# One PSUM ring for scores, transpositions, sums and broadcasts, and a query projection that is asked for first

## The chip, the core and the metric

The program runs on one core of a Trainium2 chip. TensorE (PE) multiplies matrices into PSUM, a small memory of eight banks; ScalarE (ACT) and VectorE (DVE) read the banks and write SBUF; GpSimd (POOL) does some elementwise work; SyncE's queue (SP) issues most DMAs. Each engine works through its own list of instructions in order and waits for others by semaphores. The metric is the device time of one execution in microseconds; lower is better.

## The reference

Two transformer blocks on 512 image positions and, in the second block, 256 context positions, all in float32. The first block mixes a dilated-window and a neighbourhood attention (8 heads of 64 each) and ends in a gated convolutional feed-forward layer. The second block has two layers, and each layer has three attentions, whose outputs are gated, projected and summed:

```python
    ya_l = sweep_query_blocks(lambda i, qb: dense_attend(qb, mk_all, mv_all), mq_l).reshape(b, n, BRANCH_W)
    ...
    yb_l = diff_post(sweep_query_blocks(lambda i, qb: diff_attend(qb, dk_all, dv_all, lam), dq_l),
                     diff_subln, lam_init)
    ...
    yc_l = swa_latent(sq_l, sk_l, sv_l, sk_c, sv_c, swa_sink)

    x = x + gate * merge_branches((ya_l, yb_l, yc_l), z_l, gm_l, w_branch, w_out)
```

The first (in the kernel `mla`) is dense attention of 8 heads over compressed keys. The second (`diff`) subtracts one softmax from another. The third (`swa`) has 16 heads with a window of 128 positions each way plus all of the context, and a learned sink in the softmax. In layer 0 the context's own queries are computed too; in layer 1 they are not.

## The kernel before

Activations lie transposed, 128 channels by positions. A product in float32 is done as three products of split numbers: `mm3` multiplies high by high, low by high and high by low part (L338 to L340). So a projection of 128 outputs over 1024 inputs is 24 matmuls of 512 columns, accumulated in one PSUM bank of the tag `mm`, and a function `evac` then empties it.

An attention is cut into units: one head and two tiles of 128 queries. A unit has two halves. `scores` multiplies queries by keys into banks of the tag `s`, takes the maximum, exponentiates, and scales the rows by the reciprocal sum, which leaves two tiles `p` in SBUF. `values` (L637) transposes `p` in groups of up to 512 columns: PE writes four 128x128 transpositions to a bank `t` (L657), ACT copies it to `pth` and DVE the rest to `ptl` (L381, L382). Then PE multiplies the values by `pth` and `ptl` into the bank `pv` (L675). In `swa` a unit of image queries has three score tiles (two local ones of 256 or 384 columns, L1573 on DVE, and one of both query tiles against the context, L1576) and three transposition groups; a unit of context queries has one of each.

`attend` (L420) writes the work down in this order: the first two transposition groups of the unit before, then the scores of this unit, then portions of other projections, then the products with the values and the third transposition group. The other projections are those of the next head (`mand`) and the gates of the attention (`opt`, functions `gm` and `zz` in `gates`). I call them the fill: they don't depend on the softmax that is under way. A gate `zz` waits for its head's output. When the fill of an attention is used up, what follows on PE is the merge of the branch (L1250), whose sums need every head.

This written order isn't what the engines get. The framework's scheduler goes through it with a model of durations, and takes at each point the instruction written earliest among those that are ready and whose tiles have a free buffer. Buffers of one tag form a ring with a fixed number, and are handed out in the written order. The result is one fixed list for each engine. With the tags as they stand, the eight banks are `mm` 3, `t` 1, `pv` 1 and `s` 3. The tag `t` also serves the sums over channels (`tok_sum`, L551), the tag `s` the broadcasts (`bcast`, L581), and, where `self.wide` is set, every second projection.

In `mla`, `prep` writes down a head's projections: for an even head the keys (`uk`), the values (`ux`) and then the queries (`uq`), for an odd one the queries alone. Their pages of SBUF come from a ring of 11 with the tag `hl`.

Of the kernel before, what the change touches and what calls it, by code (L numbers as in the profile page):

```python
# [9 lines left out]
F32 = mybir.dt.float32  # L10
# [8 lines left out]
P = 128  # L19
# [129 lines left out]
def _vec_layout():  # L149

    lay, off = {}, 0
    for name, n in (("c", 8), ("b_ada", 48), ("g_mix", 8), ("g_ffn", 8), ("g_final", 8), ("c_2", 8), ("c_ctx_2", 8), ("b_mod_2", 48), ("norm_g_2", 16),
                    ("mla_q_norm_2", 6), ("mla_kv_norm_2", 4), ("diff_subln_2", 2), ("final_norm_2", 8)):
        lay[name] = (off, n)
        off += n
    return lay, off
# [92 lines left out]
class Weight:  # L249


    def __init__(self, prog, name):
        self.p, (self.off, self.n), self.parts = prog, prog.U[name], {}
# [25 lines left out]
class Prog:  # L279
    def __init__(self, tc, A, out, stage=None):  # L280
        self.tc, self.nc, self.A, self.out, self.stage = tc, tc.nc, A, out, stage
        self.n = 0
        off, self.U = 0, {}
        for name, w, _ in _units():
            self.U[name] = (off, w)
            off += w * P
        self.lay, self.nvec = _vec_layout()
        self.bg, self.ahead, self.late = [], {}, []
        self.wide, self.turn = False, 0
        self.cur = None  # L290
        self.banks = dict(mm=3, t=1, pv=1, s=3)
        self.lo = self.nc.vector
        self.spare = 0

# [3 lines left out]
        return pool.tile(shape, dt, tag=tag, name=f"{tag}_{self.n}", bufs=bufs)  # L298

    def ps(self, tag):  # L300
        if tag == "mm" and self.wide:

            self.turn += 1
            tag = ("mm", "s")[self.turn % 2]
        return self.t(self.pp, [P, 512], F32, tag, self.banks[tag])

    def page(self):

# [27 lines left out]
    def mm3(self, ps, wh, wl, xh, xl, first, last):  # L336
        mm = self.nc.tensor.matmul
        mm(ps, wh, xh, start=first, stop=False)  # L338
        mm(ps, wl, xh, start=False, stop=False)  # L339
        mm(ps, wh, xl, start=False, stop=last)  # L340
# [944 lines left out]
    def mla(self, l, h, ctx):  # L1285
# [3 lines left out]
        ys, done, st = [], set(), {}  # L1289
# [3 lines left out]
        lat, gens = [], []  # L1293
        for nm, ng, tc_ in (("qc", 3, ctx), ("kvc", 2, True)):
            xs = [self.f3() for _ in range(ng)]
            gens += [self.proj(f"{nm}{l}_{i}", h, lambda ps, cs, x=xs[i]: nc.scalar.activation(x[:, cs], ps, AF.Copy),
                               ctx=tc_, back=l == 0 and tc_) for i in range(ng)]
# [40 lines left out]
        qn, kvn = nrm  # L1338
# [7 lines left out]
        def prep(j):  # L1346
            g, e = j // 2, j % 2
            gens = []
            if e == 0:
                def ev_k(ps, cs):  # L1350
                    self.split_page(kt[0], ps[:64], cs, rows=slice(0, 64))
                    self.split_page(krp, ps[64:], cs, rows=slice(64, P))
                gens.append(self.proj(f"uk{l}_{g}", kvn, ev_k, kn=2, ctx=True))
                st["v", g] = [self.page() for _ in range(2)]
                gens.append(self.v_wide(f"ux{l}_{g}", kvn, st["v", g], 2))
            q = st["q", j] = self.page()
            ys.append(self.f3())

            def ev_q(ps, cs):
                a = self.st()[:, :ps.shape[-1]]  # L1360
                if cs.start == 0:
                    nc.vector.tensor_tensor(a, ps, tab[e], op=ALU.mult)
                else:
                    nc.scalar.activation(a, ps, AF.Copy, scale=self.cmask[:, e:e + 1])
                self.split_page(q, a, cs)

            gens.append(self.proj(f"uq{l}_{j}", qn, ev_q, kn=3, ctx=ctx))
            if e:

                nc.gpsimd.tensor_copy(kt[1][64:], krp[64:])  # L1370
            return gens

        def unit(j, q0, lt):
# [11 lines left out]
            def values():  # L1385
# [4 lines left out]
                if q0 in (256, S):  # L1390
# [5 lines left out]
            return scores, values  # L1396

        heads = [(lambda j=j: prep(j), (8900 if j % 2 else 8900), [unit(j, *q) for q in self.qpairs(ctx)])
                 for j in range(KD)]
        self.run_pairs(heads[0][0]())  # L1400
# [361 lines left out]
```

## Time and profile before

| What | us |
|---|---|
| median of 3 runs | 3541.15 (3540.62 to 3547.24) |
| the profiled execution, its own time | 3543.59 |
| its span, first to last instruction | 3541.7 |
| PE busy | 3421.3 (97%) |
| DVE busy | 2357.5 (67%) |
| ACT busy | 1810.4 (51%) |
| POOL busy | 442.8 (13%) |

The profile gives for every instruction its engine, its source line, its tiles, its start and its duration. Matmuls are pipelined: each one's duration is longer than its distance to the next, so a PE that is busy all the time may still leave small gaps. Times in the rows are counted from the span's start.

### The profile page before, as it was taken

To read this page: it belongs to the slowest core of one execution; us is meant where nothing else is said; L and a number is where in the kernel's file an instruction comes from. 1 tells how busy PE (TensorE), PEld (TensorE's weight loads), DVE (VectorE), ACT (ScalarE), POOL (GpSimd) and SP (SyncE) were. 2 spreads that over 40 slices of the span, in tenths; PEclk is the share of its full clock that TensorE was granted. 3 is DMA by queue.
4 is the path that set the end of the run, shared out by engine and by line. 5 is a ranking of instruction groups with operands and counts; after the bars stand their busy time and mean duration, and the time that the engine had idled before them with its cause. 6 is when DMAs were issued, how large, how long until landed. Compare 5 with 4: busy or idle time off the path is not lost. (4 is left out here: it accounts for less than half of the span.)

```text
span 3541.7 us, 54478 instructions
## 1 busy us (share of the span) xinstructions
PE 3421.3 (97%) x19696; PEld 2926.8 (83%) x19696; DVE 2357.5 (67%) x4964; ACT 1810.4 (51%) x4162; POOL 442.8 (13%) x314
## 2 busy tenths in 40 slices
PE   6999999999999999999999999999999999999998
PEld 4787788778888988899888888888888888887777
DVE  7867678896445546566746777655565666757885
ACT  3456444423556525444525777334673555537772
POOL 3001036652001100001100001000010001000010
PEclk9999999999999999999999999999999999999999
DMA  6844445574211243322252111423114333262224
GB/s 227 261 157 117 157 155 161 165 227 138 75 57 37 60 141 90 85 75 79 56 168 89 58 51 46 145 94 99 56 50 147 111 102 84 77 183 77 63 70 142
DMA packets 200352, 392.41 MB, mean 111 GB/s; under 512 B 26290, under 2 KB 39858, under 8 KB 200083
## 3 DMA queue, kind: packets, MB, share of 16 engines
q1 hardware_dynamic: 199378, 385.23, 35.9%
q0 software_dynamic: 704, 3.70, 0.3%
q8 instruction: 155, 2.54, 0.3%
q14 instruction: 115, 0.93, 0.1%
HBM read 302.82 MB, written 38.83 MB: 96 GB/s over the span
## 5 line engine op out<-in xcount | busy, mean ns | idle before, releaser
L338 PE MATMUL mm<-h,whi 128*128 128x512 f32 (+2 forms) x2748 | 993.4, 362 | 4.2 <-ACT h L611 2.7
L339 PE MATMUL mm<-h,wlo 128*128 128x512 f32 (+2 forms) x2748 | 992.2, 361 | 5.0 <-DVE wlo L275 2.7
L340 PE MATMUL mm<-h,whi 128*128 128x512 f32 (+2 forms) x2748 | 990.1, 361 | 0.0
L274 ACT ACTIVATE whi<-wraw 128x512 fp32r<-128x512 f32 x761 | 470.2, 623 | 569.4 <-PE mm L340 338.5
L275 DVE TENSOR_TENSOR wlo<-wraw,whi 128x512 fp32r<-128x512 f32 (+2 forms) x631 | 445.0, 710 | 309.8 <-ACT whi L274 305.1
L339 PEld LDWEIGHTS mm<-h,wlo 128*128 128x128 f32 (+1 forms) x2748 | 522.0, 190 | 68.6 <-DVE wlo L275 3.3
L338 PEld LDWEIGHTS mm<-h,whi 128*128 128x128 f32 (+1 forms) x2748 | 522.0, 190 | 67.7 <-ACT h L611 3.0
L340 PEld LDWEIGHTS mm<-h,whi 128*128 128x128 f32 (+1 forms) x2748 | 521.9, 190 | 66.0
L382 DVE TENSOR_TENSOR ptl<-t,pth 128x512 fp32r<-128x512 f32 (+1 forms) x480 | 298.1, 621 | 156.4 <-ACT pth L381 151.9
L381 ACT ACTIVATE pth<-t 128x512 fp32r<-128x512 f32 (+1 forms) x480 | 260.5, 543 | 221.5 <-PE t L657 215.7
L657 PE MATMUL t<-ident,p 128*128 128x128 f32 x1680 | 287.3, 280 | 29.9 <-DVE ptl L382 19.5
L657 PEld LDWEIGHTS t<-ident,p 128*128 128x128 f32 x1680 | 195.2, 141 | 96.4 <-DVE ptl L382 44.8
L275 POOL TENSOR_TENSOR wlo<-wraw,whi 128x512 fp32r<-128x512 f32 (+1 forms) x130 | 216.9, 1684 | 262.5 <-ACT whi L274 253.3
L338 PE MATMUL mm<-hl,whi 128*128 128x512 f32 (+1 forms) x680 | 243.0, 358 | 6.3 <-ACT hl L381 5.3
L339 PE MATMUL mm<-hl,wlo 128*128 128x512 f32 (+1 forms) x680 | 240.9, 355 | 0.0
L675 PE MATMUL pv<-pth,hl 128*128 128x256 f32 (+1 forms) x1184 | 224.4, 293 | 6.0 <-ACT pth L381 4.8
L1417 POOL TENSOR_TENSOR st<-st,tab 128x512 f32<-128x512 f32 x52 | 75.1, 1444 | 1198.5 <-DMA st<-st 811.2
L675 PEld LDWEIGHTS pv<-pth,hl 128*128 128x128 f32 x1184 | 178.5, 190 | 48.8 <-ACT pth L381 34.8
L1245 POOL TENSOR_TENSOR f<-f,st 128x512 f32<-128x512 f32 x72 | 85.9, 1194 | 783.9 <-DVE st L1244 606.2
L340 PE MATMUL mm<-f,whi 128*128 128x512 f32 (+1 forms) x504 | 178.3, 355 | 0.0
L1213 ACT ACTIVATE p<-s,m 128x512 f32<-128x512 f32 x192 | 132.1, 688 | 89.9 <-DVE m L1208 88.1
L675 PE MATMUL pv<-ptl,hl 128*128 128x256 f32 (+1 forms) x768 | 169.1, 294 | 1.5 <-DVE ptl L382 1.5
(266 smaller groups left out, 6379.6 us busy)
## 6 DMA issues: line engine op xcount, KB each, us to landing
wraw<-in_wst SPq DMA_DIRECT2D x734, 256.0 KB, 2.7
mraw<-in_w_mod SPq DMA_DIRECT2D x48, 512.0 KB, 3.8
hl<-hl SPq DMA_DIRECT2D x128, 192.0 KB, 3.0
mraw<-in_w_ada SPq DMA_DIRECT2D x36, 512.0 KB, 4.6
tg<-st SPq DMA_DIRECT2D x64, 256.0 KB, 2.0
st<-st SPq DMA_DIRECT2D x208, 64.0 KB, 2.0
p<-tg SPq DMA_DIRECT2D x40, 256.0 KB, 2.8
p<-tg SPq DMA_DIRECT2D x24, 384.0 KB, 3.5
```

Of the source, the lines that this page charges most:

```text
L274: nc.scalar.activation(hi[:, :n], raw[:, :n], AF.Copy)
L275: p.lo.tensor_tensor(lo[:, :n], raw[:, :n], hi[:, :n].bitcast(F32), op=ALU.subtract)
L338: mm(ps, wh, xh, start=first, stop=False)
L339: mm(ps, wl, xh, start=False, stop=False)
L340: mm(ps, wh, xl, start=False, stop=last)
L381: nc.scalar.activation(dst_h, src, AF.Copy)
L382: nc.vector.tensor_tensor(dst_l, src, dst_h.bitcast(F32), op=ALU.subtract)
L657: self.nc.tensor.transpose(tp[:, o + i * P:o + i * P + P], pp[t][:, cols[i]:cols[i] + P], self.ident)
L675: mm(dst, sv, x_[:, o:o + w], start=first, stop=last)
L1213: nc.scalar.activation(p[:, 0:S], a[t], AF.Exp, bias=m[:, 2 + t:3 + t], accum_out=m[:, 4 + t:5 + t])
L1245: nc.gpsimd.tensor_tensor(ys[j][:, cs], ys[j][:, cs], th, op=ALU.mult)
L1417: nc.gpsimd.tensor_tensor(a, a, tab[0], op=ALU.mult)
```

## The change

The tag `t` is given up. Its tiles come from the ring of `s`, which gets the bank and has four. So six tiles of an image unit of `swa` (two transposition groups, three score tiles, a third group) go through four banks in the written order, where before three went through one and three through three. In `wide` stretches the alternation is between three banks and four. In `mla`, the page of the queries is taken before the pages of the values, and `uq` is the first of a head's projections.

```diff
-        self.banks = dict(mm=3, t=1, pv=1, s=3)
+        self.banks = dict(mm=3, pv=1, s=4)
...
     def ps(self, tag):
         if tag == "mm" and self.wide:
             self.turn += 1
             tag = ("mm", "s")[self.turn % 2]
-        return self.t(self.pp, [P, 512], F32, tag, self.banks[tag])
+        self.n += 1
+        ring = "s" if tag == "t" else tag
+        return self.pp.tile([P, 512], F32, tag=ring, name=f"{tag}_{self.n}", bufs=self.banks[ring])
...
         def prep(j):
             g, e = j // 2, j % 2
             gens = []
+            q = st["q", j] = self.page()
             if e == 0:
...
                 st["v", g] = [self.page() for _ in range(2)]
                 gens.append(self.v_wide(f"ux{l}_{g}", kvn, st["v", g], 2))
-            q = st["q", j] = self.page()
             ys.append(self.f3())
...
-            gens.append(self.proj(f"uq{l}_{j}", qn, ev_q, kn=3, ctx=ctx))
+            gens.insert(0, self.proj(f"uq{l}_{j}", qn, ev_q, kn=3, ctx=ctx))
```

The three extracts that follow are from the lists that the scheduler made, with the tiles' full names; the first number in a name is the same in both programs. They show the `swa` of layer 1 late in its course. The first is PE's list before. `s_6941` to `s_6943` are the scores of one unit, and `t_6934` is the first transposition group of the unit ahead of it, whose softmax left `p_6923` and `p_6924`; `mm_6927` is fill, a gate's projection.

```order
L675 MATMUL pv_6912_35157<-ptl_6918_35173,hl_6251_32077 128x256 x2
L1186 MATMUL s_6941_35281<-hl_6229_31911,hl_6799_34656 128x256
L1186 MATMUL s_6942_35282<-hl_6229_31911,hl_6799_34656 128x384
L1186 MATMUL s_6943_35283<-hl_6229_31911,hl_6799_34656 128x256 x2
...
L338 MATMUL mm_6927_35227<-h4_4772_24409,whi_6947_35313 128x512
L339 MATMUL mm_6927_35227<-h4_4772_24409,wlo_6948_35314 128x512
L675 MATMUL pv_6912_35157<-ptl_6933_35244,hl_6251_32077 128x128
L657 MATMUL t_6934_35262<-ident_2_69,p_6923_35188 128x128
L340 MATMUL mm_6927_35227<-h4_4772_24409,whi_6947_35313 128x512
L657 MATMUL t_6934_35262<-ident_2_69,p_6924_35189 128x128
```

Here the scores of the next unit stand ahead of the transpositions of this one, and fill stands between. The second is PE's list after the change, the same tiles:

```order
L660 MATMUL t_6934_35262<-ident_2_69,p_6924_35189 128x128
L660 MATMUL t_6937_35271<-ident_2_69,p_6924_35189 128x128
L1189 MATMUL s_6941_35281<-hl_6229_31911,hl_6799_34656 128x256
L1189 MATMUL s_6942_35282<-hl_6229_31911,hl_6799_34656 128x384
L1191 MATMUL s_6941_35281<-hl_6230_31912,hl_6799_34656 128x256
L1191 MATMUL s_6942_35282<-hl_6230_31912,hl_6799_34656 128x384
L678 MATMUL pv_6912_35157<-pth_6935_35267,hl_6252_32078 128x256 x2
L1189 MATMUL s_6943_35283<-hl_6229_31911,hl_6799_34656 128x256 x2
...
L678 MATMUL pv_6912_35157<-ptl_6951_35333,hl_6251_32077 128x128
L660 MATMUL t_6958_35365<-ident_2_69,p_6944_35292 128x128
```

Both first transposition groups now stand ahead of the next unit's scores, and no projection stands between; the lines are three higher in this program. The third is DVE's list after the change for the same unit, from its first score tile to the scaled rows. `ISA` is the reduction of a local score tile, with its accumulator read.

```order
L1577 ISA p_6944_35292,m_6940_35280<-s_6941_35281,wmask_5_75 128x256
L385 TENSOR_TENSOR ptl_6936_35268<-t_6934_35262,pth_6935_35267 128x512
L385 TENSOR_TENSOR ptl_6939_35277<-t_6937_35271,pth_6938_35276 128x512
L1577 ISA p_6945_35293,m_6940_35280<-s_6942_35282,wmask_5_75 128x384
L1580 TENSOR_REDUCE m_6940_35280<-s_6943_35283 128x2
L385 TENSOR_TENSOR ptl_6951_35333<-t_6949_35330,pth_6950_35332 128x128
L1582 TENSOR_TENSOR m_6940_35280<-m_6940_35280 128x2
L1583 TENSOR_SCALAR m_6940_35280<-m_6940_35280,sink1_6226_31906 128x2
L1596 RECIPROCAL m_6940_35280<-m_6940_35280 128x2
L1601 TENSOR_SCALAR p_6944_35292<-p_6944_35292,m_6940_35280 128x256
```

The two copies of the transposition groups stand between the unit's first score tile and its second.

## Rows read from the trace of the kernel before

**Rows 1.** The page: the span, and PE's busy time, share and instructions.

```profile
span 3541.7 us, 54478 instructions
PE 3421.3 (97%) x19696; PEld 2926.8 (83%) x19696; DVE 2357.5 (67%) x4964; ACT 1810.4 (51%) x4162; POOL 442.8 (13%) x314
```

**Rows 2.** Waits of PE, whole span: waiting line, releaser, us, times, longest.

```profile
PE t L657 <- DVE ptl L382: 19.5, 30, 1.4
PE s L586 <- DVE rstd L578: 10.4, 5, 4.9
```

**Rows 3.** Stretches: length, then busy us (instructions) of each engine, PE clock, DMA.

```profile
930.00:1245.00 315.00, 310.50 (x2025) 276.88 (x2024) 167.47 (x312) 192.22 (x436) 26.29 (x22) 1.00 0.20 59
1880.00:2250.00 370.00, 357.38 (x2271) 307.61 (x2270) 269.00 (x710) 264.63 (x727) 25.65 (x23) 1.00 0.21 62
2190.00:2250.00 60.00, 58.49 (x374) 50.19 (x373) 46.62 (x112) 40.38 (x108) 6.37 (x6) 1.00 0.30 95
3190.00:3455.00 265.00, 256.84 (x1444) 204.17 (x1443) 213.88 (x577) 201.89 (x549) 19.99 (x15) 1.00 0.23 70
3410.00:3450.00 40.00, 38.63 (x214) 29.57 (x213) 31.95 (x81) 26.57 (x74) 3.87 (x3) 1.00 0.29 86
```

**Rows 4.** Waits of PE in 1880 to 2250, then in 3190 to 3455.

```profile
PE t L657 <- DVE ptl L382: 7.9, 10, 1.2
...
PE t L657 <- DVE ptl L382: 3.6, 9, 0.7
```

**Rows 5.** Timeline of PE near 1404: start us, us, engine, line, tiles, shape, count.

```profile
1404.11 0.28 PE L371 MATMUL mm<-whi,h 128*128 128x256 f32 x1
1404.23 0.40 PE L338 MATMUL mm<-h,whi 128*128 128x512 f32 x1
1404.47 0.40 PE L339 MATMUL mm<-h,wlo 128*128 128x512 f32 x1
...
1406.80 0.60 PE L657 MATMUL t<-ident,p 128*128 128x128 f32 x4
```

**Rows 6.** Groups by shape, DVE, 3200 to 3450: busy us, mean ns, idle before.

```profile
L382 DVE TENSOR_TENSOR ptl<-t,pth 128x512 fp32r<-128x512 f32 x61 | 42.0, 688 | 15.0 <-ACT pth L381 14.5
...
L1576 DVE TENSOR_REDUCE m<-s 128x2 f32<-128x512 f32 x30 | 20.5, 683 | 0.8 <-PE s L1188 0.6
...
L1573 DVE CUSTOM_DVE_ANT_0 p<-s,wmask 128x384 f32<-128x384 f32 x29 | 16.0, 550 | 4.0 <-PE s L1188 3.8
...
L1573 DVE CUSTOM_DVE_ANT_0 p<-s,wmask 128x256 f32<-128x256 f32 x29 | 12.1, 416 | 2.5 <-PE s L1188 2.4
...
L382 DVE TENSOR_TENSOR ptl<-t,pth 128x128 fp32r<-128x128 f32 x31 | 8.9, 286 | 0.9 <-ACT pth L381 0.4
L1579 DVE TENSOR_SCALAR m<-m,sink 128x2 f32<-128x2 f32 x30 | 7.6, 252 | 0.3
```

**Rows 7.** Timelines of ACT and DVE: exponentials and scaling of one `swa` unit.

```profile
3321.57 0.28 ACT L1581 ACTIVATE m<-m,sink 128x2 f32<-128x2 f32 x1
3322.65 0.62 ACT L1587 ACTIVATE p<-p,m 128x384 f32<-128x384 f32 x1
...
3324.25 0.16 DVE L1592 RECIPROCAL m<-m 128x2 f32<-128x2 f32 x1
...
3324.50 0.91 ACT L621 ACTIVATE p<-p,m 128x256 f32<-128x256 f32 x2
```

**Rows 8.** Stretches near 465 (columns as in rows 3), and PE's timeline there.

```profile
430.00:461.00 31.00, 29.82 (x179) 26.39 (x177) 16.41 (x36) 10.30 (x18) 0.00 (x0) 1.00 0.41 129
461.00:472.00 11.00, 5.11 (x22) 4.83 (x23) 10.29 (x36) 6.08 (x15) 0.00 (x0) 0.55 0.31 92
...
461.90 0.38 PE L338 MATMUL mm<-h,whi 128*128 128x256 f32 x1 [1.99 <-ACT h L611]
468.28 1.22 PE L586 MATMUL s<-ident,rstd 128*128 128x128 f32 x4 [4.89 <-DVE rstd L578]
```

## The prediction

> **What bounds the kernel now.** I read the page's busy times first: PE works for 3421.3 of 3541.7 us [rows 1], so a change can gain at most the 120 us in which PE stands still, and part of that is the start and the end. Then PE's waits: the largest is of the transpositions (L657) for the copy that empties their one bank, 19.5 us in 30 waits; the next, of the broadcasts (L586) for DVE's `rstd`, is one for data [rows 2]. So the single bank `t` costs what can be seen as 19.5 us, of which 7.9 and 3.6 us lie in the two `swa` stages [rows 4] and 8.0 elsewhere. Then the stages: in `swa` of layer 0 PE is busy for 357.4 of 370 us, in that of layer 1 for 256.8 of 265, and in their last stretches for 58.49 of 60 and 38.63 of 40 us [rows 3]. PE has work up to the end of each, because the fill lasts that long.
>
> **What the change moves.** The two lists of PE decide this case. In every `swa` unit of the list before but a few, the scores of the next unit stand ahead of this unit's transpositions (90 of 90 score tiles in layer 1, 103 of 109 in layer 0); after the change it is none, in any stage. The ring hands out its banks in the written order, and six tiles of a unit go through four banks. So the third score tile needs the bank that the copy of the first transposition group leaves, and that group needs the softmax of its own unit. Where before the softmax of two units ran side by side, each unit now has to finish its softmax before the next unit's scores can begin.
>
> While there is fill this costs little: the scheduler puts more fill into each unit, and attention falls back in the list. Measured in PE work at the same tile, it lags by 29 us in `swa` of layer 0 and by 33 us in layer 1; in all the other attentions the lag ends within 5 us of zero. Then the fill is gone. In layer 1, from the first row of `s_6897` to the last of `s_7039`, eight units, the list after has not one projection among its rows, the list before 96. In layer 0, from `s_4445` to `s_4558`, it is 2 rows against 100. What follows is the merge, which needs all heads. There nothing hides the chain, and PE waits in each unit.
>
> **The price of a unit without fill.** I follow one image unit in the order after, from the end of the row scaling of `p_6924` to that of `p_6945`:
> - a hop and the last four transpositions, 0.60 by the row of four, together 0.65 us [rows 5];
> - the first local score tile, whose two products stand first and third of four: some 0.4 us until DVE can start, by the 0.12 us from one 256-column product to the next [rows 5] and the pipeline's end;
> - on DVE the 256-column tile, two 512-column copies, the 384-column tile: 0.42 + 2 x 0.69 + 0.55 = 2.35 us by mean durations; back to back an instruction starts about 0.08 us before the former's end, so 2.05 [rows 6];
> - the reduction of the third tile 0.68, a 128-column copy 0.29 and two small operations 0.4 [rows 6]: some 1.35;
> - ACT's exponentials to the reciprocal: from 3321.57 to 3324.25, 2.68 us [rows 7];
> - reciprocal to the end of the two scalings: 3324.25 to 3324.50 + 0.91, 1.16 us [rows 7].
>
> Sum: 8.3 us a unit. PE's own work in it is nine transpositions at 0.11, eight score products (six at 0.12, two at some 0.175) and ten value products at 0.12: 3.2 us. So PE waits for 5.1 us a unit. A context unit has one score tile and one group: 0.65 + 0.75 for its scores, a copy of the unit before in between (0.6), 1.1 for reduction and small operations, 1.4 and 1.16 for the two last steps; 5.6 us, of which PE works 1.9.
>
> Layer 1: eight intervals between units, 8 x 8.3 = 66.4 us, less the work in them (3.7 and seven times 3.2, 26.1): 40 us. Layer 0: six intervals behind image units, 49.8 less 20.1 of work, and three behind context units, 16.8 less 6.5: 40 us. Together 80 us. The idle time that these last stretches have already, 1.5 and 1.4 us [rows 3], goes off: 77.
>
> **The clock.** Near 462 us PE waited for 1.99 and 4.89 us within 11 us in which it was busy for 5.11; the granted clock of that stretch was 0.55, after 1.00, and a broadcast's four matmuls took 1.22 us instead of 0.60 [rows 5, 8], so PE was at 1.2 GHz. Waits of 5 us in each unit should bring that about. On the chain it doubles the transpositions and the scores, some 0.9 us a unit, 15 us over 17 units if it lasts through both stretches; I take half, 7.5. The Trainium skill (TensorE: Matmul & The Clock Gate, Part 1: The HAM clock gate) has it that the array runs at 1.2 GHz after idling and at 2.4 GHz after sustained work; by that the whole of both stretches would be slow, and the sum 7.5 us higher. The rows above agree in kind, and nothing here depends on the page.
>
> **What is gained.** The 8.0 us of waits for the bank `t` outside `swa` go. Of the 11.5 us inside, I count half as gone: the third score tile now waits for the same copies, in some hundred places of the list. The worst is that none goes; the best that all the 19.5 do, and the small gaps beside them that don't show as waits.
>
> **The rest.** A projection of queries asked for first moves nine matmuls (18 with context) ahead of the keys and values, and its weight's load, ACT's and DVE's split of it, and the load's place in SP's queue with it. PE has other fill there: it idles for 4.5 us in all of 930 to 1245 [rows 3]. I take 0; it can't give more than those 4.5, and if the values' copies then come late, it costs the latency of such a copy, under 3 us a layer. The fourth bank of `wide` stretches and the sums over channels in the ring: 0, since they wait for data; at most 2 us either way.
>
> **Sum.** 77 + 7.5 - 8.0 - 5.75 = 71 us over the profiled execution's 3543.6 us, 3614. That execution stands 2.4 us above the median, so 3612 us.
>
> **Rivals.**
> - *The ring does what a ring of banks is for* (faster). All waits for the bank go, and the stretches without fill cost nothing, since PE's queue holds what it needs. Time: 3541 - 19.5 = 3522. For it: the waits are real and the largest of PE. Against it: the lists, in which a unit's transpositions always stand ahead of the next scores. It decides if a unit's chain is no longer than its PE work, 3.2 us; the exponentials and scalings alone are 3.84 us [rows 7]. The Trainium skill (Perfetto Trace Analysis, Optimizing Tensor Performance: Matmuls) advises that independent matmul groups rotate through different banks, so that emptying one overlaps the next group; by it this rival would be the likely one. The waits in rows 2 agree with the rule; the order of the lists speaks against its use here. Chance 0.06.
> - *The chain is short.* Without other work between them the steps are faster, with the copies beside the chain: 6.9 us a unit (8.3 less the two copies at 0.6 and 0.2 of overlap). The 14 image intervals then cost 20 us less, the clock stays high, and all bank waits go: 77 - 20 - 19.5 = 38, so 3579. Chance 0.16.
> - *The chain is late everywhere.* Where there is fill, its own copies on ACT and DVE stand between the steps, and the scheduler's durations are too short by some 0.5 us a unit; over some 55 units ahead of the two stretches that is 28 us more, and the clock is low throughout (7.5): 3612 + 36 = 3648. It would show as many waits of transpositions for `p` in the first parts of `swa`. Chance 0.18.
> - *Nothing is to be seen.* Gains elsewhere and losses cancel, to within 0.2%, 7 us, which is about what a measurement of this kernel can tell from no change. It asks for a chain under 4.5 us. Chance 0.05.
>
> **How the numbers follow.** The forecast, 3612 with its own range of 3590 to 3635, has 0.55. The range of 0.8 takes in most of the short chain and of the late one: 3562 to 3660. Slower by over 0.2% are the forecast, the short chain and the late chain, 0.89; within 0.2%: 0.05; faster: 0.06.
>
> **What would show it.** Right: in the two last stretches of `swa`, some 66 us each, PE is busy for less than half and its transpositions wait for ACT's scaling (L621 before, L624 after) some 4 to 5 us each; the granted clock falls there; waits of transpositions for `ptl` are few; the other stages keep their lengths within 3 us. Wrong: PE is busy in those stretches as in rows 3; or the scores' third tile, not the transpositions, is what waits; or the time is lost in the dense part, or in `mla`.

## The result and the profile after

The changed kernel takes 3656.27 us (3652.28 to 3657.6, four runs), beside 3544.19 us for the kernel before on the same chip: a ratio of 1.0315, with a 95% interval of 1.0302 to 1.0328. It is 112 us slower. The forecast was 3612 us, 71 us slower, with a range up to 3660.

First the page of the kernel after: span, busy times, and the clock that PE was granted, in 40 slices of 91 us.

```profile
span 3655.8 us, 54462 instructions
PE 3460.3 (95%) x19696; PEld 2982.8 (82%) x19696; DVE 2376.7 (65%) x4964; ACT 1805.3 (49%) x4162; POOL 443.6 (12%) x314
PEclk9999999999999999999999997999999999999979
```

PE executes the same 19,696 matmuls as before and is busy for 39 us longer [rows 1]. Its clock has two dents, in the slices at the end of the two `swa` stages. Next PE's waits in the whole span (waiting line, releaser, us, times, longest), where rows 2 had the wait for the one bank of the transpositions at the top:

```profile
PE t L660 <- ACT p L624: 76.4, 43, 5.4
PE s L589 <- DVE rstd L581: 10.7, 6, 4.9
PE pv L678 <- DVE ptl L385: 7.8, 13, 2.5
```

The old wait (transpositions for `ptl`, the single bank) has left the head of the list. In its place PE's transpositions wait for ACT's scaling of the rows, four times as long. The same view, restricted to the end of `swa` in layer 0 (2195 to 2300) and in layer 1 (3470 to 3565), has most of it:

```profile
PE t L660 <- ACT p L624: 29.3, 11, 5.4
...
PE t L660 <- ACT p L624: 28.1, 9, 4.3
```

And the stretches (length, busy us and instructions of each engine, PE's clock, DMA): the two ends of `swa`, the two dense parts ahead of them, and `mla` of layer 0.

```profile
2216.70:2287.00 70.30, 41.39 (x185) 37.17 (x185) 37.98 (x107) 35.81 (x105) 2.01 (x2) 0.68 0.07 22
3477.00:3548.00 71.00, 43.43 (x204) 40.60 (x205) 38.55 (x121) 38.25 (x112) 2.54 (x2) 0.72 0.02 6
1888.00:2200.00 312.00, 300.54 (x1896) 259.66 (x1895) 214.81 (x558) 211.58 (x578) 22.91 (x19) 1.00 0.20 57
3260.00:3470.00 210.00, 203.28 (x1118) 166.79 (x1116) 159.28 (x418) 149.57 (x402) 18.23 (x12) 1.00 0.26 75
935.00:1255.00 320.00, 311.23 (x2019) 279.27 (x2018) 167.88 (x310) 191.01 (x434) 25.37 (x22) 0.99 0.20 58
```

Where before PE was busy for 58.49 of 60 us and 38.63 of 40 [rows 3] (the 60 run some 16 us into the merge; in the 70 ahead of it PE is busy for 67.55), it is now busy for 41.39 of 70.30 and 43.43 of 71.00 us, and that at a mean clock of 0.68 and 0.72. The dense parts are as before: in layer 0 11.5 us idle in 312 here, 11.1 in 310 before (370 - 357.38 less 60 - 58.49, rows 3); in layer 1 6.7 in 210 here, 6.8 in 225 before (265 - 256.84 less 40 - 38.63).

To place the whole difference I take the start of the same projection tile in both traces, at the borders of the stages (start after minus start before, so the growth within a stage is a difference of two; with another projection as the border it shifts by some us, for `mla` 1 of the changed kernel between 8 and 13):

| Kernel | `mla` 0 | `swa` 0 | `mla` 1 | `swa` 1 | at 3510 us, in all |
|---|---|---|---|---|---|
| the changed kernel | +7.5 | +47.7 | +11.0 | +43.7 | +113.8 |
| queries first, alone | +4.9 | -1.2 | +8.2 | +0.9 | +10.9 |
| changed, scores written first | +1.9 | -10.8 | +2.6 | -7.9 | -23.6 |
| changed, ring of five | +22.7 | +43.7 | +23.4 | +43.8 | +134.9 |
| `mm` 2, `t` 2 | +21.6 | -6.9 | +27.1 | -3.3 | +47.5 |
| `mm` 2, one bank unused | +22.9 | -0.2 | +35.5 | +6.0 | +77.0 |
| changed, no scaling in the last heads | +5.1 | +20.6 | +9.9 | +25.3 | +63.4 |

So 91 of the 114 us arise in `swa` and 18.5 in `mla`; `diff`, the first block and the merges have the rest.

One unit of the end of layer 1, step by step. This is the timeline of the kernel after (start, us, engine, line, tiles, shape, count), shortened to the steps of the chain:

```profile
3505.78 0.90 ACT L624 ACTIVATE p<-p,m 128x256 f32<-128x256 f32 x2
...
3506.33 1.97 PE L660 MATMUL t<-ident,p 128*128 128x128 f32 x8 [3.34 <-ACT p L624]
3507.95 0.88 PE L1189 MATMUL s<-hl,hl 128*128 128x384 f32 x2
...
3508.75 1.29 DVE L385 TENSOR_TENSOR ptl<-t,pth 128x512 fp32r<-128x512 f32 x2 [1.79 <-ACT pth L384]
...
3509.59 0.70 PE L1189 MATMUL s<-hl,hl 128*128 128x256 f32 x2
3509.96 0.55 DVE L1577 CUSTOM_DVE_ANT_0 p<-s,wmask 128x384 f32<-128x384 f32 x1
...
3510.78 0.69 DVE L1580 TENSOR_REDUCE m<-s 128x2 f32<-128x512 f32 x1
...
3512.36 0.29 ACT L1585 ACTIVATE m<-m,sink 128x2 f32<-128x2 f32 x1 [0.69 <-DVE m L1583]
...
3514.88 0.17 DVE L1596 RECIPROCAL m<-m 128x2 f32<-128x2 f32 x1
...
3515.14 0.91 ACT L624 ACTIVATE p<-p,m 128x256 f32<-128x256 f32 x2 [0.49 <-DVE m L1596]
```

The steps are scaling, transpositions, the first scores, the copies that empty the banks, DVE's reduction of the first score tile (3509.96, behind its two copies, though the products were done by 3509.37), that of the third tile (whose products begin at 3509.59, after the first of the two copies into `ptl`), exponentials, reciprocal, scaling. Each waits for one ahead of it, by data or by its engine's order. From the end of one second scaling (3505.78 + 0.90) to the next (3515.14 + 0.91) it takes 9.37 us, and PE waits 3.3 us for it.

### The profile page after: what moved, and what is told of

Same layout as the page of the kernel before. It is cut to its first block, busy times and chain, and to the rows that moved or that the text cites. A ratio compares the mean times of both kernels' runs of the same rounds, so it can differ in the third digit from the quotient of the medians.

```text
span 3655.8 us, 54462 instructions
## 1 busy us (share of the span) xinstructions
PE 3460.3 (95%) x19696; PEld 2982.8 (82%) x19696; DVE 2376.7 (65%) x4964; ACT 1805.3 (49%) x4162; POOL 443.6 (12%) x314
## 5 line engine op out<-in xcount | busy, mean ns | idle before, releaser
L343 PEld LDWEIGHTS mm<-h,whi 128*128 128x128 f32 (+1 forms) x2748 | 520.5, 189 | 70.3
L660 PE MATMUL t<-ident,p 128*128 128x128 f32 x1680 | 276.4, 292 | 90.2 <-ACT p L624 76.4
L385 DVE TENSOR_TENSOR ptl<-t,pth 128x512 fp32r<-128x512 f32 (+1 forms) x480 | 285.1, 618 | 114.6 <-ACT pth L384 110.9
L384 ACT ACTIVATE pth<-t 128x512 fp32r<-128x512 f32 (+1 forms) x480 | 244.9, 543 | 230.7 <-PE t L660 220.3
L660 PEld LDWEIGHTS t<-ident,p 128*128 128x128 f32 x1680 | 203.9, 149 | 138.0 <-ACT p L624 102.8
L1189 PE MATMUL s<-hl,hl 128*128 128x256 f32 (+2 forms) x640 | 188.9, 364 | 8.6 <-DVE ptl L385 5.7
```

The source lines that it names most:

```text
L384: nc.scalar.activation(dst_h, src, AF.Copy)
L385: nc.vector.tensor_tensor(dst_l, src, dst_h.bitcast(F32), op=ALU.subtract)
L660: self.nc.tensor.transpose(tp[:, o + i * P:o + i * P + P], pp[t][:, cols[i]:cols[i] + P], self.ident)
L1189: mm(ps, q[:, par, q_], k[:, par, k_], start=st[0], stop=False)
```

## The experiments

Ratios are to the kernel before, run beside each on the same chip, with 95% intervals.

**1. The edit on queries alone**, on the kernel before:

```diff
+            q = st["q", j] = self.page()
             if e == 0:
...
-            gens.append(self.proj(f"uq{l}_{j}", qn, ev_q, kn=3, ctx=ctx))
+            gens.insert(0, self.proj(f"uq{l}_{j}", qn, ev_q, kn=3, ctx=ctx))
```

> Before, with the queries' projection asked for first and nothing else: the ring of four is undone. My theory (the loss comes from the common ring alone, which puts each unit's transpositions ahead of the next unit's scores): 3544 us, within 4 us of before in each direction, both mla stages within 3 us of before. Rival (the later values of mla cost the 8 us and 11 us that the two mla stages grew by): 3560 to 3566 us, with the growth in the two mla stages and none in swa.

3555.01 us, 1.0033 (1.0021 to 1.0046): some 10 to 12 us, all in the two `mla` (table), between my range and the rival's. My "0" was wrong. Which half of the edit does it, experiments 9 and 10 ask.

**2. The changed kernel with the scores written first** in `attend`:

```diff
                 vals = pend() if pend else iter(())
-                next(vals, None)
                 s_()
+                next(vals, None)
```

> After, with one change: attend writes the scores of a unit down ahead of the first two transposition groups of the unit before it, so the ring of four hands its banks to the scores first. My theory (the written order of a common ring sets the order on PE, and the exposed chain is the loss): the scores stand ahead of the transpositions again, fill lasts to the end of both swa stages, and the time is 3530 to 3555 us, at most 1.004 of before. Rival (sharing banks is itself the cost, since a score tile waits for a copy in any order): still over 3600 us.

3522.47 us, 0.994 (0.9927 to 0.9952): the loss is gone, and it is faster than both kernels, by more than I expected. The ends of the two `swa` (their last transpositions start at 2220 and 3416 us), in the view of the stretches:

```profile
2150.00:2220.00 70.00, 68.09 (x453) 59.89 (x452) 56.91 (x156) 59.27 (x167) 8.48 (x7) 1.00 0.18 55
3345.00:3415.00 70.00, 67.34 (x394) 55.48 (x393) 59.99 (x171) 59.06 (x166) 8.68 (x6) 1.00 0.20 57
```

PE is busy to the end at full clock, with the same four banks. Between this kernel and the changed one only two lines have changed places. So it is the order in which the ring's tiles are written, not the ring, that made the loss.

**3. A ring of five**, with one bank less for projections:

```diff
-        self.banks = dict(mm=3, pv=1, s=4)
+        self.banks = dict(mm=2, pv=1, s=5)
```

> After, with the ring one bank larger and the projections' ring one smaller (mm 2, pv 1, s 5). The third score tile of a unit now has a bank without waiting for the copy of the first transposition group, but the written order is as it was. My theory (written order): PE's list still has every unit's transpositions ahead of the next scores, the last eight units of swa have no fill, and the time is 3640 to 3670 us. Rival (four banks are too few, the wait for the copy is the cost): under 3590 us, with swa near its length before.

3678.79 us, 1.0384 (1.037 to 1.0398), some 9 us above my range. The two `swa` lose 43.7 and 43.8 us, much as with four banks. The third score tile no longer waits for a copy: its products run together with those of the other two. But the transpositions of the unit before still stand ahead of them, and wait for the scaling:

```profile
3526.97 1.97 PE L660 MATMUL t<-ident,p 128*128 128x128 f32 x8 [3.25 <-ACT p L624]
3528.59 1.31 PE L1189 MATMUL s<-hl,hl 128*128 128x384 f32 x4
```

So one more bank does not loosen the chain, and the wait of the third score tile for its bank is not what makes it. What it loses beyond the changed kernel, 22 us, lies in `mla` (table), and experiments 4 and 7 say why: it belongs to the missing bank for projections.

**4. Two banks for the transpositions** in place of a ring, again with `mm` 2 (on the kernel before):

```diff
-        self.banks = dict(mm=3, t=1, pv=1, s=3)
+        self.banks = dict(mm=2, t=2, pv=1, s=3)
```

> Before, with two banks for t and two for mm (mm 2, t 2, pv 1, s 3), no common ring. It takes away the wait of the transpositions for their one bank, 19.5 us, without touching the order between scores and transpositions. My theory: transpositions' waits for the copy fall under 5 us, the loss of the common ring does not come, 3520 to 3545 us if two banks are enough for the projections. Rival (transpositions side by side are themselves what lengthens the stages, by keeping ACT and DVE from the softmax): over 3560 us. If two banks are too few for projections, it shows as waits of mm matmuls for ACT and DVE in the feed-forward and merge stages.

3591.12 us, 1.0133 (1.0118 to 1.0149). My expectation of a gain missed, and so would a story about the transpositions: both `swa` are faster than before, by 6.9 and 3.3 us, and the loss is in `mla`, where PE's waits between 2400 and 2800 are headed by

```profile
PE mm L369 <- DVE hl L382: 8.4, 3, 5.1
PE mm L338 <- DVE hl L382: 3.5, 2, 2.0
```

that is, projections (`mm`) for the copies that empty their banks. Experiment 7 tests this.

**5. The order of writing alone**: experiment 2's two lines on the kernel before, with its own banks and its own order of pages.

> The kernel before with its own banks and its own order of pages, and only this changed: attention writes a unit's scores ahead of the former unit's transpositions. Theory (what made the version with scores written first fast is that the ring is then harmless, and the ring itself gives what it was expected to): alone, the order of writing does next to nothing, since before the two kinds of tiles have banks of their own and the list has the scores first already; 3538 to 3550 us. Rival (the order of writing is worth as much by itself, and the ring gives nothing): 3515 to 3528 us.

3539.82 us, 0.9988 (0.9979 to 0.9997). As expected nearly nothing: 4 us of the 22. It is a sum of larger parts, though: in the traces the first block is some 9 us longer, `swa` of layer 0 some 8 us shorter and `diff` of layer 1 some 7 us shorter. Why is open.

**6. Experiment 2 with own banks**: scores first and queries first, but `t` 1 and `s` 3 again.

> The changed kernel with scores written first, but with banks of their own for transpositions (one) and scores (three), as before: only the ring is taken back. Theory (the ring is worth what that version gained beyond the cost of asking for q first): 3545 to 3560 us, some 25 to 35 us slower than with the ring, and the transpositions wait for the copy of their one bank again, some 20 us in about 30 waits. Rival (the ring gives nothing, the order of writing gives all): 3515 to 3528 us, with few such waits.

3553.18 us, 1.0026 (1.0015 to 1.0037). Against experiment 2 only the ring is missing, and the time is 31 us longer. So with queries first a ring of four is worth some 31 us, if its tiles are written in the right order. Some 13 of them are what the edit on queries costs without the ring (this run against experiment 5): against experiment 5, which has neither, experiment 2 gains 17 us. The waits that I named are there, though smaller (13.1 us in 16 waits, where I expected some 20 in 30); those of the value products stand beside them:

```profile
PE pv L675 <- ACT pth L381: 13.5, 27, 2.0
PE t L657 <- DVE ptl L382: 13.1, 16, 2.8
```

**7. Two banks for projections, one bank unused** (the kernel before with `mm=2` and nothing else).

> The kernel before with two banks for projections in place of three, one bank left unused. Theory (the loss of the kernel with two banks for transpositions came from the projections' two banks, and lies in the two latent attentions): 3585 to 3605 us, with some 20 to 27 us more in each latent attention, none in the windowed ones, and projections waiting for DVE's second half of the split that empties their bank. Rival (two banks are enough for projections, and the loss came from two groups of transpositions side by side): 3540 to 3550 us.

3621.54 us, 1.0222 (1.0207 to 1.0237). The place and the wait are as the theory has it, the size is not: 22.9 and 35.5 us in the two `mla`, 77 in all with some 13 outside the four stages of the table, where I expected 41 to 61. Thus in experiment 4 the second bank for transpositions gave back some 30 of the 77 us. PE's waits in `mla` of layer 1, 2480 to 2860:

```profile
PE mm L369 <- DVE hl L382: 8.7, 4, 5.2
PE pv L675 <- ACT pth L381: 8.2, 13, 1.7
```

**8. More work for PE in the last units** of the changed kernel, so that its clock stays high:

```diff
             if i < len(grps) - 1:
                 yield
+        if self.warm:
+            w = self.ps("mm")
+            for k in range(self.warm):
+                mm(w, parts[0][0][:, :P], parts[0][0], start=k == 0, stop=k == self.warm - 1)
...
+                self.warm = 16 if j > 5 and lt else 0
```

> The changed kernel, with 16 more matmuls of 512 columns behind the value products of each image unit of the last two heads in both windowed attentions; their sum goes into a projection bank and is read by nobody. In the list they stand where PE waits for the softmax, so they use time in which it would stand still, 3.6 us a unit at 2.4 GHz against waits of 5 to 6 us. Theory (the low clock is a part of why a unit takes 9.2 to 9.7 us and not the 8.3 of the prediction): the granted clock stays near 1.00 in the last units, a unit takes 8.2 to 8.7 us, and the time falls to 3632 to 3646 us. Rival (the chain on ACT and DVE is longer by itself, the clock does not matter): the clock rises, the units keep their 9.2 to 9.7 us, 3650 to 3660 us. Second rival (the added matmuls delay the transpositions behind them): over 3665 us.

3682.28 us, 1.0384 (1.0369 to 1.0398): slower than the changed kernel by 26 us, the second rival. The clock did stay high at the end of layer 1, from 3505 us on, yet the units there start 8.38 to 10.19 us apart, 9.4 on average, no less than in the changed kernel. The stretches, and then the timeline of one border between units:

```profile
3520.00:3540.00 20.00, 19.66 (x111) 16.25 (x109) 11.92 (x36) 12.28 (x35) 1.60 (x1) 1.00 0.10 27
3540.00:3560.00 20.00, 19.64 (x110) 16.08 (x108) 13.77 (x38) 11.54 (x33) 1.59 (x1) 1.00 0.16 46
```

```profile
3526.88 2.27 PE L687 MATMUL mm<-pth 128*128 128x512 f32 x9
...
3527.20 0.91 ACT L624 ACTIVATE p<-p,m 128x256 f32<-128x256 f32 x2
...
3528.99 1.03 PE L660 MATMUL t<-ident,p 128*128 128x128 f32 x8
3529.78 0.54 PE L1193 MATMUL s<-hl,hl 128*128 128x256 f32 x2
```

Eight transpositions and the way to the scores now take 0.79 us (3528.99 to 3529.78) where the changed kernel needed 1.62 at the low clock (3506.33 to 3507.95): 0.83 us, which is what the clock costs at this step in a unit that is slow throughout it. But the added matmuls hold the transpositions up for longer: PE comes to them 0.88 us after the scaling's end (3528.11), where in the unit above they began 0.35 us before it. The edit also moved the fill in the list: some 40 matmuls of projections stand between 3505 and 3550, where the changed kernel has none, and the units without fill came earlier, with PE waiting as before:

```profile
3480.00:3500.00 20.00, 11.06 (x56) 10.15 (x57) 10.82 (x36) 11.74 (x35) 0.00 (x0) 0.79 0.00 0
```

So this run measures the step and not the whole; a time at full clock with nothing else changed was not had. Of the 26 us some 13 arose in `swa` of layer 1 and some 12 by the end of that of layer 0 (at the same projection near 2310 us it is 67.7 us behind the kernel before, the changed kernel 55.7), the two stages to which matmuls were added.

**9 and 10. The two halves of the edit on queries**, each alone on the kernel before: the page asked for first, or the projection put first.

> The kernel before, with only the first half of the edit on queries: q's page is asked for first, its projection stays last. Theory (the edit costs some 11 us because the nine or eighteen matmuls of the projection, with their load and copies, go ahead of keys and values, whose copies then come late): the page alone costs nothing, 3540 to 3548 us. Rival (the page handed out earlier makes others wait for pages): 3550 to 3560 us.

> The kernel before, with only the second half of the edit on queries: the projection of queries goes ahead of those of keys and values, its page is asked for where it was. Theory (the place of the projection costs): 3550 to 3560 us, with 4 to 6 us more in the latent attention of layer 0 and 8 to 10 in that of layer 1, and value products that wait for the copies of the transposed probabilities. Rival (the order of pages costs): 3540 to 3548 us.

The page alone: 3541.07 us, 0.9999 (0.9989 to 1.0008). The projection's place alone: 3554.62 us, 1.0038 (1.0024 to 1.0051). So the place costs all of it. In `mla` of layer 1 (2420 to 2760) PE's longest waits in sum with the projection first, and the stretch itself, first before and then with the projection first:

```profile
PE pv L675 <- ACT pth L381: 3.4, 4, 1.4
PE t L657 <- DVE ptl L382: 2.2, 4, 0.9
```

```profile
2420.00:2760.00 340.00, 336.91 (x1928) 288.30 (x1928) 201.72 (x389) 195.36 (x421) 23.77 (x16) 1.00 0.31 91
```

```profile
2420.00:2760.00 340.00, 331.30 (x1902) 284.72 (x1901) 194.49 (x373) 189.55 (x401) 23.42 (x16) 0.99 0.29 86
```

PE idles for 8.7 us in place of 3.1, and its longest wait in sum is that of the value products for copied probabilities.

**11. No scaling of rows** in the last two heads of both `swa` of the changed kernel:

```diff
-                for t in range(2):
+                for t in range(0 if j > 5 else 2):
                     r = m[:, 10 + t:11 + t]
```

> The changed kernel without the scaling of the rows by the reciprocal of their sums in the last two heads of both windowed attentions; this part of the computation is left out there. Theory (in the last units each step waits for the one before, from copies to scaling): a step of 1.16 us less in each of 17 to 20 units, and no more waits of transpositions for the scaling; 3630 to 3640 us, the last stretches 50 to 60 us long in place of 70. Rival (what is late there is the banks, handed out by DVE's copies, and the softmax runs beside them): 3650 to 3658 us.

3607.1 us, 1.0187 (1.0173 to 1.0201): 49 us less than the changed kernel, twice what I expected, and the rival (banks, not the chain) falls. The step of 1.16 us was taken out, and the image units of the last heads of layer 1 start 6.1 to 7.5 us apart in place of 9.4. The reciprocal and the small operations ahead of it no longer stand in the chain either, transpositions can begin after the first of two exponentials, and PE stays longer at 2.4 GHz (0.88 in the mean from 3440 to 3510 us):

```profile
3440.00:3510.00 70.00, 54.34 (x280) 44.08 (x279) 43.85 (x137) 39.81 (x121) 3.85 (x3) 0.88 0.10 31
```

How the 2.6 us divide among these three was not measured.

**12. Queries second**, behind keys and ahead of values, in experiment 2's kernel (`gens.insert(1, ...)`):

> The version with the ring and scores written first, with the projection of queries put behind that of keys and ahead of that of values, in place of first of all. Theory (the place of the projection costs with the ring too, some 2 us in the latent attention of layer 0 and 3 in that of layer 1, and keys first takes back most of it): 3516 to 3520 us against 3522.5. Rival (with the ring the place no longer matters, since the scores' banks, not the values' copies, set the pace there): 3520 to 3526 us. Second rival (the values' copies come later still behind both): 3528 us or more.

3523.29 us, 0.994 (0.9925 to 0.9955), the same as experiment 2: my theory missed, and the first rival held. With scores written first the ring hides what the place costs: in experiment 2's kernel `mla` grows by 1.9 and 2.6 us, not by 4.9 and 8.2. The ring without any edit on queries was not tried.

## Why the prediction was right, and where it was off

- **The order of the list was the cause, as said.** Experiments 2 and 3 part it from the number of banks: two lines exchanged take 134 us off the median, a fifth bank takes nothing off in `swa`. Experiment 11 shows that in the last units each step waits for the one before.
- **The fill is gone at the end, and there the loss arises.** The two stretches are 70.3 and 71.0 us long, where I said some 66 each. Against the rival of a chain that is late everywhere stands the dense part, whose idle time has not grown; against the short chain stand the 9.4 us of a unit.
- **The price of a unit was too low.** Eight intervals in layer 1, from first scores to first scores (3471.01 to 3546.18 us), have a mean of 9.4 us against my 8.3. In layer 0 PE's last projections end at 2214.6 us; the eight intervals from 2211.00 to 2282.99, six behind image units and two behind context units, take 72.0 us, for which my terms give 61.0. In the unit above, by my own steps: hop and transpositions 1.27 us against 0.65; from the first scores to the reduction 2.83 against 2.45; reduction to exponentials 1.58 against 1.35; exponentials to the reciprocal 2.52 against 2.68; reciprocal to the end of scaling 1.17 against 1.16. The first of these steps is more than half of the difference, and by experiment 8 it is the clock; over the eight units of layer 1 it has a mean of 1.17 us.
- **The clock was sized at half of both stretches, and the rows show little more.** Mean clocks of 0.68 and 0.72 are 1.2 GHz in 64 and 56% of the time. The two levels alternate within a unit; of the one above, these are a part in which PE works and one in which it waits:

```profile
3505.50:3511.50 6.00, 5.17 (x23) 5.17 (x24) 4.14 (x11) 2.37 (x6) 0.00 (x0) 0.50 0.01 3
3512.50:3515.00 2.50, 0.00 (x0) 0.00 (x0) 0.44 (x3) 2.15 (x9) 0.00 (x0) 1.00 0.00 0
```

So the low part often falls on the work behind the wait: in six of the eight units of layer 1 the eight transpositions take 1.55 us or more from the first start to the last, against 0.89 in the unit at 3497.60. For the sum of the units the full 15 us would have been nearer than 7.5, but the part of the clock in the whole excess was not measured. "PE busy for less than half" was a bad sign to look for: at 1.2 GHz the same matmuls keep PE busy longer, so its share is 59 and 61% though it waits in each unit, and most of these waits are 3.3 us, where I said 4 to 5. The Trainium skill's section on the HAM clock gate (TensorE: Matmul & The Clock Gate, Part 1) has the array slow after idling. The trace agrees in kind, by the slow transpositions behind those waits. What I took from it, that both stretches would be slow from end to end, did not come: that would be a mean of 0.50, and 0.68 and 0.72 lie nearer to the 0.75 of my half.
- **The gain of 5.75 us inside `swa` did not come.** The waits for the one bank (7.9 and 3.6 us, rows 4) are gone, and others, for ACT's scaling, 7.3 and 5.2 us in the dense parts, are there in their place.
- **The gain of 8.0 us elsewhere did not come, and the edit on queries was not free.** In `mla`, where I wrote 0, the stages grew by 7.5 and 11.0 us: one of my signs of being wrong, time lost there, is present beside those of being right. Experiment 10 puts some 12 us of that to the projection's place. I had named the mechanism (value copies that come late) and bounded it at 3 us a layer by the latency of one such copy; but it recurs, four times in layer 1, and the scores and transpositions behind it are late too.

In sum: `swa` 91 us against 79 (77 + 7.5 - 5.75), and the rest 22 us against -8. The direction and the main place were right. Of the 43 us between forecast and profile 30 are what I gave to the other stages, and some 12 lie in `swa`. There the longer units make 12 (19.8 over the 16 intervals, less the 7.5 for the clock) and the gain that did not come 6 more; some 5 us the other way are not placed.

The measured 3656 us lies outside the forecast's own range, 3590 to 3635. The wide range reaches it only because it takes in most of the late chain, whose cause, a longer dense part, did not come. That it reached so far was luck.

The Trainium skill (Perfetto Trace Analysis, Optimizing Tensor Performance: Matmuls) advises that independent groups rotate through different banks, so that emptying one overlaps the next. The 31 us between experiments 6 and 2 agree with it. But a unit's scores don't depend on the transpositions of the unit before, and still the same four banks made the changed kernel 112 us slower. So these runs add a condition: a tile that waits for a long chain must not be written ahead of one that needn't wait for it.

## What to carry to other kernels

A ring of buffers that several kinds of tiles share is also an order: read, in the order in which its tiles are written, whether a tile that is needed early stands behind one that waits for a long chain, and move the early one ahead before counting banks. Look for the loss where independent work has run out, and price a unit there by its whole chain, with TensorE at the low clock for the work behind each wait. Test an edit that only reorders projections by itself: here it cost some 12 us that no wait in the profile before announced.

## What the runs showed of the hardware that I had not expected

The clock fell again and again in stretches in which PE was busy for 59 and 61% of the time, and came back within the same unit. Since eight transpositions with the way to the scores then take 1.62 us and not 0.79, the fall hides in the busy time: PE's total rose by 39 us with the same 19,696 matmuls. And in this kernel one bank of three for projections is worth more than a second for the transpositions: without it the kernel takes 77 us longer, while the second bank `t` gave back some 30, though the single one was the longest wait in PE's list.
